# A two-layer fp32 transformer trunk on one core: the low part of twelve weight tiles by an accumulating transfer, a tenth Strassen pair, and one shared PE visit

## The chip, the cores and the metric

The kernel runs on one core of one Trainium2 chip. The metric is the device time of one execution in microseconds (us), as the median of several runs; lower is better. A core has a matrix engine (PE, with its weight loads listed as PEld), three engines for elementwise work (VectorE = DVE, ScalarE = ACT, GpSimd = POOL), a queue engine that starts loads (SyncE = SP), and 16 DMA engines. Each engine works through its own list of instructions in order, and waits for semaphores of the others.

## The reference

An input of 256 tokens by 1024 features goes through two layers; all of it is float32.

```
for i in range(DEPTH):                      # DEPTH = 2
    if i == 0: mix = moba_attention(h, ...) # 16 heads of 64; one block of 256, so plain causal attention here
    else:      mix = dilated_attention(h, ...)   # 3 groups of 4 heads: dilation 1, 4, 16, windows 128, 512, 2048
    h = layer_norm(ALPHA * h + mix, ...)
    h = layer_norm(ALPHA * h + square(relu(h @ w_in)) @ w_out, ...)   # w_in 1024x4096, w_out 4096x1024
```

Each attention has its q, k and v projections, rotary turns of q and k, scores, a softmax, the weighted sum of v (PV) and an output projection.

## The kernel before

**Arithmetic.** A float32 product is made of three products of fp32r parts: each operand is split into a high part (`hi`, a rounded copy) and a low part (`lo = x - hi`), and hi·hi + lo·hi + hi·lo is summed in PSUM. So every weight tile needs three things before PE can read it: its load, a copy to `whi`, and a subtraction into `wlo`.

**Weights.** A weight tile is 128x1024 float32, 512 KB. `load_w` (L402) starts its load on SP into a slot of `raw` (6 slots), has ACT make `whi` (L377, in `split`), and then has DVE make `wlo` as `raw - whi` (L382). `whi` and `wlo` have ten slots each (`NSLOT`), and in the first MLP chunks may also borrow the slots of the LayerNorm tiles `g` and `b`.

**MLP.** The 4096 hidden columns are taken in eight chunks of 512 (chunk 0 has a token-major head of its own). A chunk loads four tiles of `w_in`, `mm_wide` fills four PSUM tiles `tp`, and `relu_sq_T` makes the squared ReLU of them on ACT and DVE, split again into `ahi` and `alo` (or into `rhi`/`rlo` and `v`/`e`/`pt`, which are lent as homes). The products with `w_out` run in two blocks per layer, after chunk 3 and after chunk 7, and add into four PSUM tiles `acc`. A block is a list of steps (`BLOCKS`, L296): "2A" is chunk 2, first pair of `w_out` tiles, as a Strassen pair; "31" is chunk 3, second pair, plain. A plain tile is 12 matmuls of 128x512 (`mm_rows`, two halves of the tokens by six). A Strassen pair (`load_pair` L858, `mm_pair` L882) forms sums of the two tiles on DVE (`m<-raw,raw`, `raw<-m,raw`, `raw<-raw`), splits each of those, and runs seven products of three matmuls, 21 in place of 24. Its activations need sums too (`side_sums` L829). `settle` (L915) puts the four side tiles together with the residual. The last tiles of a layer (`TAIL`) are held back and run row half by row half, so that the LayerNorm of the first half starts while PE still works on the second.

**Attention.** `score` (L663) runs a PE visit of scores for four heads or head groups; `turned` (L718) transposes the softmax on PE (L729); `pv_causal` (L759) and `pv_dilated` (L794) run a PE visit of PV; `attn_out` (L749) copies its result into `ahi` and `alo`. In layer 0 the PV of one unit is already run at the start of the next unit's `score` visit. In layer 1 the PV of each of the two units is a visit of its own. The order of the steps is written out in `ORDER0` and `ORDER1`.

**LayerNorm.** `ln_half` (L940) sums and normalises one half of the tokens on DVE and ACT, with a small power on POOL (L1003), and PE transposes the result four blocks at a time (L712) into the tiles `xs` for the next projection.

**Order.** No order is written by hand inside an engine. `Plan` records every operation with a guessed cost, works out a due time for each backwards from PE's order, adds the corrections of `NUDGE` (a table from operation number to a shift of its due time), and schedules a list per engine. SP's loads keep the order in which they were recorded.

Of the kernel before, what the change touches and what calls it, by code (L numbers as in the profile page):

```python
# [29 lines left out]
TAIL = (5, 6, 6, 7)  # L30
NSLOT = 10
TURN = 0.06
DVE1 = (1, 3)
# [5 lines left out]

STAGE_HOME = (("raw", 6),) * 4 + (("g", 1), ("b", 1)) + (("tok", 2),) * 2  # L40
NWARM = 7
# [10 lines left out]

BURST, RATES = 18.0, (380e3, 270e3)


def latency(p, q):
    if p.eng in ("SP", "AQ"):
        return LANDED
    if p.eng == "PE":
        return 0.0 if q.eng == "PE" else PE_OUT  # L60
    return PE_IN if q.eng == "PE" else LATS.get((p.eng, q.eng), LAT)
# [31 lines left out]
class Plan:  # L93
# [47 lines left out]
    def order(self):  # L141
# [76 lines left out]
        while len(done) < total:  # L218
# [40 lines left out]
            for b in o.bufs:  # L259
                if o.eng != "PE":  # L260
                    b.reader = o
                b.left -= 1
                b.last = max(getattr(b, "last", 0.0), o.end + (PE_OUT if o.eng == "PE" else LAT))
                if not b.left:
                    slots[b.tag].append(b.last)
# [29 lines left out]
AHEADLN = (3.0, 1.5, 4.5)  # L295
BLOCKS = ({3: "00 1A 01 1B 2A 31 2B 3A", 7: "4A 4B 5A 51 6A 61 70 71"}, {3: "00 01 1A 1B 2A 2B 3A 3B", 7: "4A 4B 5A 51 6A 61 70 71"})  # L296
WPAIRS = [
# [7 lines left out]
NUDGE = {  # L305
# [7 lines left out]
}  # L313
# [3 lines left out]
def tile_trunk(  # L317
# [41 lines left out]
    def psum(tag):  # L359
        return mk([P, 512], F32, tag, 4, ps_pool)  # L360

    def f32(ap):
        return ap.bitcast(F32)
# [29 lines left out]
    def landing():  # L393
        return mk([P, 1024], F32, "raw", 6)

# [5 lines left out]

    def load_w(src, n=1024):  # L402
        w = W()
        w.raw = landing()
        w.hi, w.lo = slot()
        dma(lambda: w.raw.t[:, :n], src[:, :n], (), [(w.raw, 0)], P * n * 4)
        split(
            n, lambda: w.raw.t[:, :n], lambda: w.hi.t[:, :n], lambda: w.lo.t[:, :n],
            [(w.raw, 0)], [(w.hi, 0)], [(w.lo, 0)], sbuf=True,
        )  # L410
        return w
# [251 lines left out]
    def score(pss, qk, blocks, first=None):  # L663

        hi, lo = qk
        before, needs, extra = first(pss) if first else (lambda: None, [], 0.0)

        def go():
            before()
            for i in range(max(len(bl) for bl in blocks)):  # L670
                for h in range(2):
                    for t, (a, b) in enumerate(((hi, hi), (hi, lo), (lo, hi))):
                        for n, bl in enumerate(blocks):
                            if i >= len(bl):
                                continue
                            qc, kc, off = bl[i]
                            r = slice(32 * n, 32 * n + 32)
                            mm(pss[n].t[:, off : off + kc.stop - kc.start], a.t[r, h, 0, qc], b.t[r, h, 1, kc],
                               h + t == 0, h + t == 3)

        cost = 0.22 + sum(6 * max((bl[i][1].stop - bl[i][1].start) / 2400 + 0.0135, 0.109) for i, bl in
                          enumerate([max(blocks, key=lambda b: b[0][1].stop - b[0][1].start)] * 2))
        op("PE", cost + extra, go, [(t, h) for t in qk for h in range(2)] + needs, pss)
# [34 lines left out]
    def turned(blocks, r, on_dve=(), first=None):  # L718
# [11 lines left out]

        op("PE", 0.2 + extra + TURN * len(blocks), go, list(r) + [ident] + needs, pss)
        pt = mk([P, 16, P], F32, "pt", 1)
# [60 lines left out]

    def pv_dilated(e, v, vcs, ahi, alo, ahead):  # L794
        r = [t for row in e for t in row]

        def blk(h, m, c):
            return lambda: e[m][h].t[:, c : c + P]

        pt = turned(  # L800
            [blk(h, m, kb * P) for kb in range(2) for h in range(2) for m in range(2)]
            + [blk(h, m, c) for c in (S, S + P) for m in range(2) for h in range(2)], r, DVE1,
        )
        o, o2 = psum("tp"), psum("tp")

        def go():
            for kb in range(2):
                weigh(o, 0, v[0][kb], vcs[0], pt, (4 * kb, 4 * kb + 2), S, 0, kb == 0, kb == 1)
            for m in range(2):
                weigh(o, S, v[1][m], vcs[1], pt, (8 + 2 * m, 9 + 2 * m), P, m * P, True, True)  # L810
                weigh(o2, 0, v[2][m], vcs[2], pt, (12 + 2 * m, 13 + 2 * m), P, m * P, True, True)

        op("PE", 0.2 + 2 * 0.432 + 4 * 0.22, go, [t for x in v for t in x] + [pt], [o, o2], ahead=ahead)
        attn_out(o, 0, 2, ahi, alo, 0, False)
        attn_out(o2, 0, 1, ahi, alo, 2, False)
# [264 lines left out]
    class Mlp:  # L1080
# [17 lines left out]
        def rest(self, between):  # L1098
# [20 lines left out]
            def wide_block(steps):  # L1119
# [3 lines left out]
                for c, n in ((int(x[0]), int(x[1], 16) % 10) for x in steps):  # L1123
# [7 lines left out]
                    else:  # L1131
                        for k in range(2):
                            item = ((*chunks[c], j + k), load_w(wout[i][pos + k]), pos + k, nkt)
                            if nkt - pos - k <= ntail:
                                tail.append(item)
                                continue
                            for m in range(2):
                                mm_rows(acc[m], item, m)
# [26 lines left out]
    def layer0(between):  # L1165
# [93 lines left out]
        pieces = [(o, P * i) for i in range(4)]  # L1259
        op("PE", 0.2 + cost, lambda: go(pieces), needs, [o])  # L1260
        causal_out(pieces, *to)
# [19 lines left out]
    def layer1(between):  # L1281
# [3 lines left out]
        quads = (((0, 0), (0, 1)), ((0, 2), (1, 0)), ((1, 1), (1, 2)))  # L1285
        qk, units, seen = {}, {}, [None, None]
        for step, a in (x.split("-") for x in ORDER1.split()):
# [8 lines left out]
            elif step == "s":  # L1296
                blocks, pss = [], []
                for u, gi in quads[n]:
# [6 lines left out]
                    for h in range(2):  # L1305
# [3 lines left out]
                        else:  # L1309
                            blocks.append([(halves[m], halves[m], m * P) for m in range(2)])  # L1310
                score(pss, qk.pop(n), blocks)
                for i, (u, gi) in enumerate(quads[n]):
# [25 lines left out]
            else:  # L1338
                e, st, sm = units[n]
                vs, vcs = [], []  # L1340
                for gi in range(NG):
                    pair = n * NG + gi
                    vs.append(V1[0] if pair < 4 else V1[1])
                    vcs.append(pair * P if pair < 4 else (pair - 4) * P)
                pv_dilated(e, vs, vcs, *attn[n], AHEAD1[n])
        items = [((*attn[j // 3], j % 3), load_w(wo1[j]), j, 6) for j in range(6)]
# [129 lines left out]
```

## Time and profile before

| | before |
|---|---|
| time, median of 3 runs | 546.71 us (546.37 to 547.74) |
| the profiled execution | 546.42 us |
| its span, first to last instruction | 544.6 us |
| PE busy | 535.7 us, 98% |
| DVE busy | 509.1 us, 93% |
| ACT busy | 365.3 us, 67% |
| POOL busy | 8.7 us, 2% |

The span is read as time on an axis that begins with the first instruction; a row of a timeline gives the start on that axis, the length, the engine, the line and the tiles (written<-read), and how many instructions of the kind it joins. Matmuls overlap, so the time of one is read from start to start of the next and not from its length. "tp", "acc", "wlo" and so on are tile names without the number of the buffer.

### The profile page before, as it was taken

What the parts mean: (1) busy time and instruction counts of PE and PEld (TensorE: products, weight loads), DVE (VectorE), ACT (ScalarE), POOL (GpSimd) and SP (SyncE); (2) the same over time, 40 slices, a digit from 0 to 9 for tenths busy, and PEclk for the clock granted to TensorE, in tenths of its full rate; (3) what the DMA queues carried; (4) which work ended last, traced back from release to release, by engine and by line L of the source; (5) the groups of instructions that cost most, each with busy time, mean ns of one, the idle gap of its engine ahead of it and who ended that gap; (6) DMA issues with size and microseconds to landing.
All of it is one profiled execution on the core that took longest, in us unless ns stands there. A gap on an engine that the chain in (4) does not pass through costs nothing.

```text
span 544.6 us, 9103 instructions
## 1 busy us (share of the span) xinstructions
PE 535.7 (98%) x3416; PEld 455.0 (84%) x3416; DVE 509.1 (93%) x866; ACT 365.3 (67%) x599; POOL 8.7 (2%) x13
## 2 busy tenths in 40 slices
PE   8999999999999999999999999999999999999994
PEld 6888888888888888888888988878888888888884
DVE  6899999797999989899999999899899999999997
ACT  6767776477976666796843557555896656888540
POOL 0000000010000000000010000000000000000001
PEclk9999999999999999999999999999999999999998
DMA  8995345738353678444853833455933358942622
GB/s 317 394 319 165 121 149 180 247 120 305 130 181 101 199 284 325 154 123 186 296 206 113 332 122 106 147 189 158 338 123 116 115 156 259 359 156 78 232 77 78
DMA packets 30396, 105.65 MB, mean 194 GB/s; under 512 B 3344, under 2 KB 4368, under 8 KB 30352
## 3 DMA queue, kind: packets, MB, share of 16 engines
q1 hardware_dynamic: 29952, 104.87, 55.6%
q8 instruction: 27, 0.44, 0.3%
q10 hardware_dynamic: 400, 0.20, 0.1%
q14 instruction: 17, 0.14, 0.1%
HBM read 104.01 MB, written 1.05 MB: 193 GB/s over the span
## 4 chain that ended last, share of the span: by engine, by line
PE 97%; DMA 1%; DVE 1%; ACT 0%; issue 0%; SPq 0%; DVEq 0%
PE tp L386 47%; PE acc L386 47%; PE tp L712 1%; PE tp L729 1%; DMA raw<-in_xw_dram 1%; DVE tok L627 0%; ACT whi L377 0%; SPq L373 0%; ACT xs L377 0%; DVE bst L964 0%; DVE tok L620 0%; DVEq L1470 0%; DVE mv L999 0%
## 5 line engine op out<-in xcount | busy, mean ns | idle before, releaser
L377 ACT ACTIVATE whi<-raw 128x1024 fp32r<-128x1024 f32 (+2 forms) x186 | 188.2, 1037 | 56.3 <-PE acc L386 15.7
L382 DVE TENSOR_TENSOR wlo<-raw,whi 128x1024 fp32r<-128x1024 f32 (+2 forms) x186 | 217.1, 1196 | 4.4 <-ACT whi L377 3.9
L386 PE MATMUL tp<-xs,whi 128*128 128x512 f32 x448 | 105.4, 390 | 0.0
L386 PEld LDWEIGHTS tp<-xs,whi 128*128 128x128 f32 x448 | 83.2, 188 | 16.8
L386 PE MATMUL acc<-xs,whi 128*128 128x512 f32 (+1 forms) x240 | 56.4, 380 | 0.8 <-ACT whi L377 0.7
L386 PEld LDWEIGHTS tp<-xs,wlo 128*128 128x128 f32 x448 | 56.0, 191 | 1.3
L386 PE MATMUL tp<-xs,wlo 128*128 128x256 f32 x448 | 56.4, 283 | 0.0
L386 PE MATMUL acc<-whi,ahi 128*128 128x512 f32 (+1 forms) x136 | 53.5, 394 | 0.0
L386 PE MATMUL acc<-wlo,ahi 128*128 128x512 f32 (+1 forms) x136 | 52.9, 389 | 0.0
L386 PEld LDWEIGHTS acc<-xs,whi 128*128 128x128 f32 x240 | 42.8, 188 | 10.3 <-ACT whi L377 1.7
L386 PE MATMUL acc<-whi,alo 128*128 128x512 f32 (+1 forms) x136 | 47.9, 388 | 0.0
L1057 ACT ACTIVATE ta<-tp 128x256 f32<-128x256 f32 x56 | 20.8, 379 | 21.2 <-PE tp L386 19.8
L620 DVE TENSOR_TENSOR ta<-tp,ta 128x256 f32<-128x256 f32 (+1 forms) x60 | 25.4, 437 | 7.9 <-ACT ta L1057 7.5
L386 PE MATMUL acc<-xs,wlo 128*128 128x256 f32 x224 | 31.7, 283 | 0.0
L386 PE MATMUL tp<-whi,e 128*128 128x512 f32 x90 | 31.2, 390 | 0.0
L386 PEld LDWEIGHTS acc<-whi,ahi 128*128 128x128 f32 x136 | 25.5, 188 | 5.5 <-issue 0.3
L386 PEld LDWEIGHTS acc<-whi,alo 128*128 128x128 f32 x136 | 25.5, 188 | 5.3
L386 PEld LDWEIGHTS acc<-xs,wlo 128*128 128x128 f32 x224 | 29.3, 191 | 0.6
L386 PEld LDWEIGHTS acc<-wlo,ahi 128*128 128x128 f32 x136 | 25.6, 188 | 5.0
L386 PE MATMUL acc<-whi,xs 128*128 128x512 f32 (+1 forms) x112 | 28.8, 365 | 0.0
L377 ACT ACTIVATE whi<-m 128x1024 fp32r<-128x1024 f32 x19 | 20.1, 1057 | 10.9 <-DVE m L620 9.2
L698 ACT ACTIVATE e<-e,mx 128x256 f32<-128x256 f32 (+2 forms) x40 | 19.8, 500 | 9.1 <-DVE mx L688 9.1
(151 smaller groups left out, 907.0 us busy)
## 6 DMA issues: line engine op xcount, KB each, us to landing
raw<-in_win_dram SPq DMA_DIRECT2D x64, 512.0 KB, 4.6
raw<-in_wout_dram SPq DMA_DIRECT2D x64, 512.0 KB, 4.5
raw<-in_wqk_dram SPq DMA_DIRECT2D x24, 512.0 KB, 5.9
raw<-in_wo_dram SPq DMA_DIRECT2D x14, 512.0 KB, 4.3
raw<-in_wv_dram SPq DMA_DIRECT2D x8, 512.0 KB, 8.3
g<-in_lng_dram SPq DMA_DIRECT2D x4, 512.0 KB, 7.3
b<-in_lnb_dram SPq DMA_DIRECT2D x4, 512.0 KB, 7.2
raw<-in_wv1a_dram SPq DMA_DIRECT2D x4, 512.0 KB, 5.4
```

Of the source, the lines that this page charges most:

```text
L377: op("ACT", act(n, sbuf=sbuf), lambda: nc.scalar.activation(hi(), src(), AF.Copy), r, whi, keen=keen)
L382: lambda: nc.vector.tensor_tensor(lo(), src(), f32(hi()), op=ALU.subtract), list(r) + list(whi), wlo,
L386: nc.tensor.matmul(out_ap, lhsT, rhs, start=start, stop=stop)
L620: op("DVE", dve(n) + extra, lambda: nc.vector.tensor_tensor(out_ap(), a(), b(), op=alu), r, w)
L698: lambda: nc.scalar.activation(e(), e(), AF.Exp, bias=bias(), scale=-1.0, accum_out=total()), r, w,
L712: nc.tensor.transpose(ps.t[:, c : c + P], src(), ident.t)
L729: nc.tensor.transpose(ps.t[:, 32 * i : 32 * i + 32], src()[c, :], ident.t[c, c])
L1057: op("ACT", act(S), lambda one=one, ps=ps: nc.scalar.activation(one(), ps.t[:, S:], AF.Copy), [ps], [uk[i]])
```

## The change

Four things change.

- **Blocks.** In layer 0 the step "31" becomes "3B", and the order of the last four steps changes. So one more pair of `w_out` tiles is a Strassen pair.
- **`load_w(..., by_dma)`.** For the plain pairs inside the blocks, 12 tiles in all ("00", "01" and "51" of each layer), `wlo` is no longer made by DVE. ACT writes the negated copy `-hi` into `wlo`, and POOL starts a transfer from `raw` to `wlo` in SBUF that adds as it writes. `raw` is held until the transfer has landed.
- **`pv_dilated(..., held)`.** In layer 1 the PV of the first unit is kept back and run at the start of the `score` visit of step "s-2", into the upper halves of three of its four PSUM tiles. `attn_out` then runs on three pieces of 256 columns instead of one of 512 and one of 256.
- **The planner.** Costs and rates that it assumes change, and `NUDGE` is a new table; all rows behind the first PE visits of layer 0 may stand elsewhere.

The counts of instructions by the order of the program: PE's matmul rows are three fewer by the pair; ACT 558 to 574, DVE 860 to 858, POOL 18 to 30, SP 210 to 210.

```diff
 NSLOT = 10
+NRAW = 6
+BY_DMA = (0, 1)
...
-BURST, RATES = 18.0, (380e3, 270e3)
+BURST, RATES = 18.0, (380e3, 340e3)
+SWDGE, ADDING = 0.9, 1.65
...
 def latency(p, q):
-    if p.eng in ("SP", "AQ"):
+    if p.xfer:
         return LANDED
...
-BLOCKS = ({3: "00 1A 01 1B 2A 31 2B 3A", 7: "4A 4B 5A 51 6A 61 70 71"}, {3: "00 01 1A 1B 2A 2B 3A 3B", 7: "4A 4B 5A 51 6A 61 70 71"})
+BLOCKS = ({3: "00 1A 01 1B 2A 2B 3A 3B", 7: "4A 4B 5A 51 6A 61 70 71"}, {3: "00 01 1A 1B 2A 2B 3A 3B", 7: "4A 4B 5A 51 6A 61 70 71"})
...
 NUDGE = {
-    221: 42.3, 258: 3.2, 275: 51.6, 799: 23.2, 810: 29, 890: 31, 1067: -6, 1076: 4.2, 1150: 55.7, 1239: 31.3, 1349:
...
+    389: 7.9, 399: -6.05, 413: 8.1, 422: 21.4, 460: 3.85, 521: 19.65, 523: 2.05, 541: -7.05, 659: -15.65, 660:
...
-    def load_w(src, n=1024):
+    def load_w(src, by_dma=False):
         w = W()
         w.raw = landing()
         w.hi, w.lo = slot()
-        dma(lambda: w.raw.t[:, :n], src[:, :n], (), [(w.raw, 0)], P * n * 4)
-        split(
-            n, lambda: w.raw.t[:, :n], lambda: w.hi.t[:, :n], lambda: w.lo.t[:, :n],
-            [(w.raw, 0)], [(w.hi, 0)], [(w.lo, 0)], sbuf=True,
-        )
+        dma(lambda: w.raw.t, src, (), [(w.raw, 0)], P * 4096)
+        raw, hi, lo = (lambda: w.raw.t), (lambda: w.hi.t), (lambda: w.lo.t)
+        if by_dma:
+            op("ACT", act(1024, sbuf=True), lambda: nc.scalar.activation(hi(), raw(), AF.Copy), [(w.raw, 0)], [(w.hi, 0)])
+            op("ACT", act(1024, sbuf=True), lambda: nc.scalar.activation(lo(), raw(), AF.Copy, scale=-1.0),
+               [(w.raw, 0)], [(w.lo, 0)])
+            op("POOL", SWDGE, lambda: nc.gpsimd.dma_start(f32(lo()), raw(), accum_op=ALU.add),
+               [(w.raw, 0)], [(w.lo, 0)], xfer=P * 4096 * ADDING)
+        else:
+            split(1024, raw, hi, lo, [(w.raw, 0)], [(w.hi, 0)], [(w.lo, 0)], sbuf=True)
         return w
...
-    def pv_dilated(e, v, vcs, ahi, alo, ahead):
+    def pv_dilated(e, v, vcs, ahi, alo, ahead, held):
...
+        needs, cost = [t for x in v for t in x] + [pt], 2 * 0.432 + 4 * 0.22
+        if held is not None:
+            held.append((go, needs, cost, ahi, alo))
+            return
...
-                            item = ((*chunks[c], j + k), load_w(wout[i][pos + k]), pos + k, nkt)
+                            item = ((*chunks[c], j + k), load_w(wout[i][pos + k], k in BY_DMA and nkt - pos > ntail), pos + k, nkt)
...
-                score(pss, qk.pop(n), blocks)
+                if held:
+                    go, needs, cost, *to = held.pop()
+                    pieces = [(ps, S) for ps in pss[:3]]
+                    score(pss, qk.pop(n), blocks, lambda _: (lambda: go(pieces), needs, cost))
+                    for j, piece in enumerate(pieces):
+                        attn_out(*piece, 1, *to, j, False)
+                else:
+                    score(pss, qk.pop(n), blocks)
...
-                pv_dilated(e, vs, vcs, *attn[n], AHEAD1[n])
+                pv_dilated(e, vs, vcs, *attn[n], AHEAD1[n], held if n == 0 else None)
```

Three places show how rows move. The first is PE at the LayerNorm of layer 1's attention, first half of the tokens (`tok_123`): the rows at the end of the output projection (`acc`), the LayerNorm's transposes, and the first rows of the MLP that read `xs`. Before:

```order
L386 MATMUL acc_749_4288<-whi_744_3973,ahi_608_4292 128x512
L386 MATMUL acc_749_4288<-wlo_745_4264,ahi_608_4292 128x512
L386 MATMUL acc_749_4288<-whi_744_3973,alo_609_4298 128x512
L712 MATMUL tp_753_4374<-ident_49_87,tok_123_345 128x128 x4
L712 MATMUL tp_754_4381<-ident_49_87,tok_123_345 128x128 x4
L386 MATMUL tp_769_4390<-whi_756_4004,xs0_1_75 128x512
```

And the same place of the changed program:

```order
L717 MATMUL tp_758_4395<-ident_49_87,tok_123_342 128x128 x4
L386 MATMUL acc_754_4321<-whi_749_3995,ahi_615_4311 128x512
L386 MATMUL acc_754_4321<-wlo_750_4263,ahi_615_4311 128x512
L386 MATMUL acc_754_4321<-whi_749_3995,alo_616_4317 128x512
L717 MATMUL tp_759_4406<-ident_49_87,tok_123_342 128x128 x4
L386 MATMUL tp_774_4414<-whi_761_4029,xs0_1_75 128x512
```

The last three matmuls of the projection, which were ahead of both groups of transposes, now stand between them.

The second place is PE in layer 1 where the first unit's PV runs (`tp<-pt,v`). Before, it stands between rows of the v projection (`acc<-whi,xs`), and the scores of step "s-2" (`tp<-rhi`) come a dozen rows later:

```order
L386 MATMUL acc_719_3975<-wlo_702_3735,xs0_1_75 128x256
L386 MATMUL tp_713_4006<-pt_712_3979,v_599_3385 64x256 x2
L386 MATMUL tp_713_4006<-pt_712_3979,v_699_3990 64x256 x2
L386 MATMUL tp_713_4006<-pt_712_3979,v_599_3385 64x128 x2
L386 MATMUL tp_714_4013<-pt_712_3979,v_599_3385 64x128 x2
L386 MATMUL tp_713_4006<-pt_712_3979,v_699_3990 64x128 x2
L386 MATMUL tp_714_4013<-pt_712_3979,v_699_3990 64x128 x2
L386 MATMUL acc_719_3975<-whi_701_3672,xs0_1_75 128x256
```

Changed:

```order
L386 MATMUL acc_713_4002<-whi_711_3669,xs1_2_76 128x256 x4
L386 MATMUL tp_720_4041<-pt_719_4005,v_606_3407 64x256 x2
L386 MATMUL tp_720_4041<-pt_719_4005,v_706_4009 64x256 x2
L386 MATMUL tp_721_4046<-pt_719_4005,v_606_3407 64x128 x2
L386 MATMUL tp_722_4049<-pt_719_4005,v_606_3407 64x128 x2
L386 MATMUL tp_721_4046<-pt_719_4005,v_706_4009 64x128 x2
L386 MATMUL tp_722_4049<-pt_719_4005,v_706_4009 64x128 x2
L386 MATMUL tp_720_4041<-rhi_691_3998 128x128
L386 MATMUL tp_721_4046<-rhi_691_3998 128x128
```

The scores follow the PV directly and share its PSUM tiles.

The third place is ACT in the second block of layer 1, where the two tiles of "51" are made ready (`raw_1076` and `raw_1079`); L409 is the copy, L410 the negated copy:

```order
L409 ACTIVATE whi_1077_5751<-raw_1076_5628 128x1024
L1065 ACTIVATE ta_1037_5763<-tp_1032_5618 128x256
L1065 ACTIVATE ta_1037_5763<-tp_1033_5630 128x256
L1067 ACTIVATE ta_1037_5763<-ta_1037_5763 128x2x256
L409 ACTIVATE whi_1080_5782<-raw_1079_5645 128x1024
L377 ACTIVATE e_1013_5790<-ta_1012_5592 128x512
L410 ACTIVATE wlo_1078_5797<-raw_1076_5628 128x1024
L410 ACTIVATE wlo_1081_5802<-raw_1079_5645 128x1024
L1065 ACTIVATE ta_1038_5817<-tp_1035_5683 128x256
```

POOL's transfers into `wlo_1078` and `wlo_1081` can start behind these two negated copies; PE reads `wlo_1078` for the first time in this row, 30 matmuls of 128x512 behind the first read of `wlo_1071`, the DVE row that follows the input of `e_1013` directly on DVE:

```order
L386 MATMUL tp_1040_5778<-wlo_1071_5785,e_990_5648 128x512
L386 MATMUL tp_1040_5778<-whi_1070_5728,e_991_5654 128x512
L386 MATMUL acc_786_4905<-whi_1072_5740,ahi_970_5545 128x512
...
L386 MATMUL acc_786_4905<-whi_1077_5751,ahi_970_5545 128x512
L386 MATMUL acc_786_4905<-wlo_1078_5797,ahi_970_5545 128x512
```

Before, the low parts of these two tiles were subtractions on DVE.

More of the change, by code (lines that the diff above doesn't have):

```diff
@@ L38 @@
 NFIRST = 4
-STAGE_HOME = (("raw", 6),) * 4 + (("g", 1), ("b", 1)) + (("tok", 2),) * 2
+STAGE_HOME = (("raw", NRAW),) * 4 + (("g", 1), ("b", 1)) + (("tok", 2),) * 2
 NWARM = 7
@@ L262, in order @@
                 b.left -= 1
-                b.last = max(getattr(b, "last", 0.0), o.end + (PE_OUT if o.eng == "PE" else LAT))
+                b.last = max(getattr(b, "last", 0.0), o.end + (LANDED if o.xfer else PE_OUT if o.eng == "PE" else LAT))
                 if not b.left:
@@ L393, in landing @@
     def landing():
-        return mk([P, 1024], F32, "raw", 6)
+        return mk([P, 1024], F32, "raw", NRAW)
     def slot():
@@ L679, in go @@
                                h + t == 0, h + t == 3)
-        cost = 0.22 + sum(6 * max((bl[i][1].stop - bl[i][1].start) / 2400 + 0.0135, 0.109) for i, bl in
+        cost = 0.42 + sum(6 * max((bl[i][1].stop - bl[i][1].start) / 2400 + 0.0135, 0.109) for i, bl in
                           enumerate([max(blocks, key=lambda b: b[0][1].stop - b[0][1].start)] * 2))
@@ L729, in go @@
                     nc.tensor.transpose(ps.t[:, 32 * i : 32 * i + 32], src()[c, :], ident.t[c, c])
-        op("PE", 0.2 + extra + TURN * len(blocks), go, list(r) + [ident] + needs, pss)
+        op("PE", 0.4 + extra + TURN * len(blocks), go, list(r) + [ident] + needs, pss)
         pt = mk([P, 16, P], F32, "pt", 1)
@@ L803, in pv_dilated, with go @@
         )
-        o, o2 = psum("tp"), psum("tp")
[L806 to L813, printed above, removed]
+        def go(pieces):
+            for kb in range(2):
+                weigh(*pieces[0], v[0][kb], vcs[0], pt, (4 * kb, 4 * kb + 2), S, 0, kb == 0, kb == 1)
+            for m in range(2):
+                for i in (1, 2):
+                    weigh(*pieces[i], v[i][m], vcs[i], pt, (4 + 4 * i + 2 * m, 5 + 4 * i + 2 * m), P, m * P, True, True)
+        needs, cost = [t for x in v for t in x] + [pt], 2 * 0.432 + 4 * 0.22
+        if held is not None:
+            held.append((go, needs, cost, ahi, alo))
+            return
+        o, o2 = psum("tp"), psum("tp")
+        op("PE", 0.4 + cost, lambda: go([(o, 0), (o, S), (o2, 0)]), needs, [o, o2], ahead=ahead)
         attn_out(o, 0, 2, ahi, alo, 0, False)
@@ L1259, in layer0 @@
         pieces = [(o, P * i) for i in range(4)]
-        op("PE", 0.2 + cost, lambda: go(pieces), needs, [o])
+        op("PE", 0.4 + cost, lambda: go(pieces), needs, [o])
         causal_out(pieces, *to)
@@ L1285, in layer1 @@
         quads = (((0, 0), (0, 1)), ((0, 2), (1, 0)), ((1, 1), (1, 2)))
-        qk, units, seen = {}, {}, [None, None]
+        qk, units, seen, held = {}, {}, [None, None], []
         for step, a in (x.split("-") for x in ORDER1.split()):
```

9 rows, old and new, of the table NUDGE are left out of this document.

## The prediction

> **What bounds the kernel now.** I read the page first: busy shares, then the chain that ended last.
>
> ```profile
> span 544.6 us, 9103 instructions
> PE 535.7 (98%) x3416; PEld 455.0 (84%) x3416; DVE 509.1 (93%) x866; ACT 365.3 (67%) x599; POOL 8.7 (2%) x13
> PE 97%; DMA 1%; DVE 1%; ACT 0%; issue 0%; SPq 0%; DVEq 0%
> ```
>
> PE is both the busiest engine and 97% of the chain. DVE at 93% is close behind, which matters only where it makes PE wait. So the next view is a window from PE's first real product to its last.
>
> ```profile
> 8.04:537.39 529.35, 529.24 (x3385) 451.07 (x3385) 501.57 (x847) 361.79 (x593) 6.92 (x7) 1.00 0.56 195
> ```
>
> The columns are the length, PE, PEld, DVE, ACT, POOL, granted clock, DMA share. Of 529.35 us PE shows 0.11 idle, at a granted clock of 1.00. Ahead of it lie 8.04 us until the first input is there, behind it 544.6 - 537.39 = 7.2 us of the last LayerNorm half. The rows of both programs are the same in these two pieces, so the time goes with the length of PE's list plus whatever PE waits inside it. A matmul's row overlaps the next, so a short wait hides in "busy"; the spacing of starts tells it. The unit of price is in the chain:
>
> ```profile
> 176.67 0.68 PE tp L386 x3
> ```
>
> Three matmuls of 128x512 take 0.68 us, 0.227 each. Against that spacing I went through PE's timeline in order of time. The visible waits are at the LayerNorms' transposes:
>
> ```profile
> 117.20 0.60 PE L712 MATMUL tp<-ident,tok 128*128 128x128 f32 x4
> 117.56 0.48 PE L386 MATMUL tp<-whi,xs 128*128 128x512 f32 x1
> 117.87 0.60 PE L712 MATMUL tp<-ident,tok 128*128 128x128 f32 x4
> 118.49 0.51 PE L386 MATMUL tp<-whi,xs 128*128 128x512 f32 x1
> ...
> 289.36 1.03 PE L712 MATMUL tp<-ident,tok 128*128 128x128 f32 x8
> 290.31 0.96 PE L386 MATMUL acc<-whi,xs 128*128 128x512 f32 x3
> ...
> 364.67 1.29 PE L712 MATMUL tp<-ident,tok 128*128 128x128 f32 x8
> 366.01 0.50 PE L386 MATMUL tp<-whi,xs 128*128 128x512 f32 x1
> ```
>
> Four transposes without a wait take 0.36 from start to the next start (117.20 to 117.56); so eight should take 0.72. The second four take 0.62 (0.26 too many), the eight at 289.36 take 0.95 (0.23 too many), the eight at 364.67 take 1.34 (0.62 too many). Together 1.11 us. At 364.67 the row behind them reads `xs`, which ACT writes late, since two weight copies are ahead of it in its queue:
>
> ```profile
> 363.46 2.01 ACT L377 ACTIVATE whi<-raw 128x1024 fp32r<-128x1024 f32 x2 [4.17 <-PE acc L386]
> 365.38 0.57 ACT L377 ACTIVATE xs<-tp 128x512 fp32r<-128x512 f32 x1
> ```
>
> **The change part by part.** *The tenth pair* takes 24 matmuls to 21: 3 x 0.227 = **-0.68 us**, on PE's list and so on the end.
>
> *The shared visit.* What a visit costs beyond its matmuls is in the timeline of layer 1:
>
> ```profile
> 337.06 0.28 PE L386 MATMUL acc<-wlo,xs 128*128 128x256 f32 x1
> 337.27 1.96 PE L386 MATMUL tp<-pt,v 128*64 128x256 f32 x24
> 339.15 0.39 PE L386 MATMUL acc<-whi,xs 128*128 128x256 f32 x1
> 339.38 0.28 PE L386 MATMUL acc<-wlo,xs 128*128 128x256 f32 x1
> 339.49 0.28 PE L386 MATMUL acc<-whi,xs 128*128 128x256 f32 x1
> ```
>
> Rows of 256 columns follow each other by 0.12 or 0.11 (339.38, 339.49); into the visit it takes 0.21 (337.06 to 337.27), out of it 0.23 (339.15 to 339.38). So a visit costs 0.09 + 0.11 = 0.20 in changes of shape, and one visit fewer is **-0.20 us**. The change from PV to scores inside the visit could give back between 0 and all of it; layer 0 already joins them without a row of its own for that, so I take the whole.
>
> *The LayerNorms.* The order of rows splits two groups of eight into fours with other PE work between them (layer 1's attention LayerNorm is shown above: three matmuls, 0.68 us, between) and puts more rows ahead of the others. At 364.67 the wait was 0.62, less than the 0.68 of the inserted rows; at 289.36 it was 0.23 and there are now several matmuls; at 117.87 it was 0.26, and by the count of rows since the last row of the projection the second transposes come some two matmuls (0.44) later. Each wait is shorter than what now covers it: **-1.11 us**. If the transposes only move with their input, nothing is gained: the bound on the other side is 0. I take the full gain, since the LayerNorm's own work on DVE is the same. Each split costs a change of shape: up to 0.20 by the visit above, near 0 by the x4 group above (its 0.36 holds its entry); three splits, **+0.10**.
>
> *DVE.* What the pair adds and the transfers take away:
>
> ```profile
> L382 DVE TENSOR_TENSOR wlo<-raw,whi 128x1024 fp32r<-128x1024 f32 x180 | 214.2, 1219 | 3.9 <-ACT whi L377 3.5
> L382 DVE TENSOR_TENSOR wlo<-m,whi 128x1024 fp32r<-128x1024 f32 x19 | 23.2, 1220 | 0.1
> L620 DVE TENSOR_TENSOR m<-raw,raw 128x1024 f32<-128x1024 f32 x19 | 23.2, 1219 | 0.0
> L620 DVE TENSOR_TENSOR raw<-raw 128x512 f32<-128x512 f32 x19 | 13.0, 686 | 0.1
> L620 DVE TENSOR_TENSOR raw<-m,raw 128x512 f32<-128x512 f32 x19 | 13.0, 686 | 0.0
> L382 DVE TENSOR_TENSOR v<-raw,v 128x512 fp32r<-128x512 f32 x19 | 12.9, 686 | 0.8 <-ACT v L377 0.8
> L382 DVE TENSOR_TENSOR e<-ta,e 128x512 fp32r<-128x512 f32 x15 | 10.3, 687 | 0.2
> L620 DVE TENSOR_TENSOR ta<-ta 128x128 f32<-128x128 f32 x38 | 10.9, 288 | 0.7
> L620 DVE TENSOR_TENSOR ta<-ta 128x256 f32<-128x256 f32 x19 | 8.0, 420 | 0.2
> ```
>
> A pair needs 1.22 + 1.22 + 3 x 0.686 + 0.687 + 2 x 0.288 + 0.42 = 6.2 us of DVE; twelve subtractions fewer are 12 x 1.219 = 14.6. DVE ends some 8.4 us lighter, about 92%. None of that is on the end by itself. ACT gains twelve negated copies, and about 2.3 us for the pair:
>
> ```profile
> L377 ACT ACTIVATE whi<-raw 128x1024 fp32r<-128x1024 f32 x180 | 185.4, 1056 | 52.7 <-PE acc L386 15.7 <-DMA raw<-in_win_dram 8.3 <-issue 6.8
> ```
>
> 12 x 1.056 + 2.3 = 15 us: 365 becomes 380 of 544, 70%. Cover is PE's list. Where it is gone is seen by how near DVE already runs to PE in layer 1's second MLP:
>
> ```profile
> 500.82 1.22 DVE L382 TENSOR_TENSOR wlo<-raw,whi 128x1024 fp32r<-128x1024 f32 x1
> ...
> 502.52 0.39 PE L386 MATMUL tp<-wlo,ahi 128*128 128x512 f32 x1
> ```
>
> This low part is done at 502.04 and read at 502.52: half a microsecond to spare, without a wait. All rows there have a new order, so some such place may come up short. Before has none in the MLPs, so 0 is the near end; the far end I set at 2 us, twice the LayerNorms' waits; I take **+0.4**, near the row.
>
> *The transfers.* This trace has no accumulating transfer. The nearest rows are the loads of the same size:
>
> ```profile
> raw<-in_wout_dram SPq DMA_DIRECT2D x64, 512.0 KB, 4.5
> raw<-in_wo_dram SPq DMA_DIRECT2D x14, 512.0 KB, 4.3
> raw<-in_wv_dram SPq DMA_DIRECT2D x8, 512.0 KB, 8.3
> ```
>
> From issue to landing 4.3 to 8.3 us; I take 4.5, the same tiles' own load. Queued behind the wait: on POOL only later transfers (the next LayerNorm's power stands behind the block's last transfer, which lands before PE is through with it); on SP the twelve loads that need a `raw` slot held by a transfer, and all loads behind them. Only 8.3 of the 52.7 us that ACT idles before its copies was ended by the loads of `w_in`, so loads mostly run ahead, and I cost that at 0. PE waits if its cover is shorter than the transfer. The eight tiles of "00" and "01" are made long before their step. Tightest are the tiles of "51". In layer 1 the negated copy ends about when DVE ends `wlo_1071` (ACT's `e` and negated copy beside DVE's subtraction), and PE reads `wlo_1078` 30 matmuls behind `wlo_1071`: 30 x 0.227 = 6.8 us. In layer 0 PE reads `wlo_553` 25 matmuls (5.7 us) after `whi_547`, whose copy ended at least one DVE subtraction (1.2) sooner, and two ACT copies (2.1) lie between: at least 4.8 us. At 4.5 both are covered: **0**. At 8.3 they would be short by 1.5 and up to 3.5.
>
> The Trainium skill, "DMA: Bandwidth & Descriptors", section "Anatomy of one DMA — SWDGE (gpsimd) path", fits a transfer issued by GpSimd as 2.0 us plus bytes over 436 GB/s, by which an estimate for 512 KB is 3.2 us, less than each row here; no run here shows it yet, and the fit is not said to be of one that adds. By it the sum would be the same 0.
>
> The sum from the profiled execution: 546.42 - 0.68 - 0.20 - 1.11 + 0.10 + 0.4 = 544.93. That execution was 0.29 below the median of 546.71, within the spread of the three runs. **I predict 544.9**, for the likeliest case 543.9 to 545.6.
>
> **The rivals.** *(1) Only the list gets shorter.* The LayerNorm's waits move with their input or come back at new places: 546.42 - 0.68 - 0.20 = 545.5, with the small stalls 545.9, and by the median's offset up to 546.2. For it: the same DVE work is in front of the transposes, and ACT has more copies that can stand ahead of `xs`, as at 363.46. Against it: the inserted rows are as long as the waits were.
>
> *(2) The transfer is slower than its cover.* If a transfer that reads and adds takes t us to land, PE waits t - 6.8 at layer 1's "51" and t - 4.8 (at most) at layer 0's. Slower begins 0.3% or 1.64 us above the median (about what a measurement of this kernel can tell from no change), at 548.35, so at 3.4 us of waits: t of 7.5 if layer 0's cover is its least, 9 if it is as long as 8. At t = 12 the waits are 5.2 and 4 to 7: 554 to 557. For it: the wv loads took 8.3, and DMA is at 0.56 of its engines; it has to read where it writes, and POOL issues it. Against it: the other two rows quoted are 4.3 and 4.5, the latter the load of these very tiles. The Trainium skill, "SBUF — State Buffer", section "Who interferes with whom", gives a way into it: GpSimd, which writes the descriptors, is locked out while a DVE copy or tensor_scalar holds the ports they share in a two-port mode. By that page tensor_tensor has no such mode, and DVE's rows quoted above for the blocks are TENSOR_TENSOR, so by it the lock is rare at "51"; no run here shows it.
>
> *(3) DVE or ACT falls behind in layer 1.* The new order leaves less to spare than the half microsecond at 502.04: two or three waits of one subtraction each (1.22) give 544.5 + 2.4 to 3.7 = 547 to 548.2, no change that can be told.
>
> **How the numbers follow.** Forecast 0.52, (1) 0.25, (2) 0.13, (3) 0.10. Most of the forecast's own range, and little else, lies more than 0.3% (545.07) below the median: faster 0.45. Its upper end, (1), most of (3) and a mild (2) are within 0.3%: 0.41. The rest of (2) and a little of (3) are slower: 0.14. The range of 543.9 to 548.4 takes in the forecast, (1), (3) and a mild (2); what it leaves out is most of (2) and the odd better case.
>
> **What would show it.** PE's count of matmuls three fewer. One row of 24 PV matmuls that runs into the scores without rows of `acc` between. The transposes of layer 1's attention LayerNorm as two groups of four, each 0.36 to the next start. Transfers into `wlo` that land in about 4.5 us, and no gap of PE at "51". DVE near 501 us, ACT near 380. I am wrong if PE's idle time in its window grows beyond a microsecond, above all with a DMA as its releaser, or if the transposes still take 0.6 to 1.3 us.

## The result, and the profile after

| | before | changed |
|---|---|---|
| median | 546.54 us (546.10 to 547.74, 6 runs) | 550.4 us (549.88 to 551.21, 6 runs) |
| ratio | | 1.0071, 95% interval 1.006 to 1.0083 |
| profiled execution, its span | 546.42, 544.6 us | 550.36, 548.3 us |

The change makes the kernel 0.7% slower, some 3.9 us. The forecast was 544.9 us, in a range up to 548.4.

The page of the changed kernel, its busy shares, the chain that ended last, and two rows of its DMA issues (the last column is the median from issue to landing):

```profile
span 548.3 us, 9149 instructions
PE 535.8 (98%) x3413; PEld 453.7 (83%) x3413; DVE 502.4 (92%) x864; ACT 378.4 (69%) x615; POOL 18.8 (3%) x25
PE 75%; DVE 10%; DMA 6%; ACT 4%; issue 3%; SPq 0%; POOL 0%; DVEq 0%; ACTq 0%
...
raw<-in_wout_dram SPq DMA_DIRECT2D x64, 512.0 KB, 4.8
...
wlo<-raw POOLq DMA_DIRECT2D x12, 512.0 KB, 8.0
```

PE has three matmuls fewer, DVE went from 509.1 to 502.4, ACT from 365.3 to 378.4: the sizes forecast. But PE is only 75% of the chain now, and DMA and DVE have entered it. The window from PE's first real product to its last says the same:

```profile
7.83:540.66 532.83, 529.39 (x3382) 449.72 (x3382) 494.93 (x845) 374.96 (x609) 17.02 (x19) 1.00 0.61 205
```

It is 3.48 us longer than before (529.35), at the same clock, and PE is idle 3.44 us of it, where it was 0.11. Behind the window lie 7.6 us, where it was 7.2: DVE's last row ends 3.54 us ahead of the end of the span, 3.15 before. In the later runs of this program it is 3.46 to 3.54 wherever there are transfers, short ones too, and 3.14 in the one that has none. So some 0.4 us at the end come with the transfers; the prediction had this piece unchanged.

What PE waited for, from the view of its waits (total, times, longest):

```profile
PE acc L386 <- DMA wlo<-raw: 2.4, 1, 2.4
PE tp L386 <- PEq L1476: 0.8, 1, 0.8
PE acc L386 <- ACT whi L377: 0.6, 1, 0.6
PE tp L717 <- DVE tok L632: 0.5, 1, 0.5
PE tp L717 <- issue: 0.4, 1, 0.4
PE tp L386 <- ACT ta L934: 0.2, 1, 0.2
```

The 0.8 is the start, as before. The largest is a transfer. PE's timeline there, in step "51" of layer 1:

```profile
513.78 0.39 PE L386 MATMUL acc<-whi,ahi 128*128 128x512 f32 x1
516.56 0.50 PE L386 MATMUL acc<-wlo,ahi 128*128 128x512 f32 x1 [2.39 <-DMA wlo<-raw]
516.89 0.39 PE L386 MATMUL acc<-whi,ahi 128*128 128x512 f32 x1
```

From start to start 2.78 and then 0.33 in place of twice 0.227: 2.66 us lost at one row. It is the second tile of the step, `wlo_1081`. The chain of waits shows its transfer, and the row of SP an issue right behind its landing:

```profile
505.33 11.19 DMA wlo<-raw
516.51 0.04 issue
516.56 2.79 PE acc L386 x11
```

```profile
516.53 0.33 SPq L373 DMA_DIRECT2D raw<-in_wout_dram  x1
```

The transfer took 11.19 us and landed at 516.51 (505.33 + 11.19); 0.02 us later SP could issue the load that needed the `raw` slot. The first tile's transfer, issued at 504.38, took 6.7 and landed as PE came to it; SP's next load went out at that moment, too. In layer 0 the two transfers of "51" took 7.0 and 8.7 us and landed in time, but the loads behind them went out only then (257.26 and 260.48) and were late. ACT's timeline shows it, and PE's some 15 us later, at the LayerNorm of the first MLP:

```profile
264.17 1.06 ACT L377 ACTIVATE whi<-raw 128x1024 fp32r<-128x1024 f32 x1 [1.32 <-DMA raw<-in_wout_dram]
266.82 1.06 ACT L377 ACTIVATE whi<-raw 128x1024 fp32r<-128x1024 f32 x1 [1.59 <-DMA raw<-in_wout_dram]
```

```profile
280.80 0.39 PE L386 MATMUL acc<-whi,alo 128*128 128x512 f32 x1
281.67 0.66 PE L717 MATMUL tp<-ident,tok 128*128 128x128 f32 x4 [0.48 <-DVE tok L632]
282.08 0.48 PE L386 MATMUL acc<-whi,rhi 128*128 128x512 f32 x1
```

0.87 from start to start in place of 0.23: the LayerNorm's DVE work stood behind subtractions that had waited for loads. That makes two theories. **T**: the accumulating transfers land too late, and cost twice, at the row that reads the low part and by the `raw` slot they hold until they land. **O**: the new order of rows is at fault, and would wait in any case.

### The profile page after: what moved, and what is told of

It reads as the page before. It is cut to its first block, busy times and chain, and to the rows that moved or that the text cites. A ratio compares the mean times of both kernels' runs of the same rounds, so it can differ in the third digit from the quotient of the medians.

```text
span 548.3 us, 9149 instructions
## 1 busy us (share of the span) xinstructions
PE 535.8 (98%) x3413; PEld 453.7 (83%) x3413; DVE 502.4 (92%) x864; ACT 378.4 (69%) x615; POOL 18.8 (3%) x25
## 4 chain that ended last, share of the span: by engine, by line
PE 75%; DVE 10%; DMA 6%; ACT 4%; issue 3%; SPq 0%; POOL 0%; DVEq 0%; ACTq 0%
PE acc L386 37%; PE tp L386 36%; DVE wlo L382 4%; DMA wlo<-raw 4%; ACT whi L377 2%; PE tp L717 1%; DVE raw L625 1%; DMA raw<-in_wout_dram 1%; DVE m L625 1%; PE tp L734 1%; DMA raw<-in_xw_dram 1%; DVE ta L625 1%; DVE tok L632 1%; ACT wlo L410 1%; DVE v L382 0%
## 5 line engine op out<-in xcount | busy, mean ns | idle before, releaser
L377 ACT ACTIVATE whi<-raw 128x1024 fp32r<-128x1024 f32 (+2 forms) x174 | 176.5, 1036 | 64.2 <-DMA raw<-in_win_dram 15.3
L382 DVE TENSOR_TENSOR wlo<-raw,whi 128x1024 fp32r<-128x1024 f32 (+2 forms) x174 | 203.7, 1196 | 11.6 <-ACT whi L377 8.4
L386 PE MATMUL tp<-whi,e 128*128 128x512 f32 x96 | 33.1, 390 | 0.0
L377 ACT ACTIVATE whi<-m 128x1024 fp32r<-128x1024 f32 x20 | 21.2, 1061 | 12.4 <-DVE m L625 12.3
L625 DVE TENSOR_TENSOR m<-raw,raw 128x1024 f32<-128x1024 f32 x20 | 24.4, 1222 | 3.9 <-DMA raw<-in_wout_dram 3.9
L386 PE MATMUL tp<-whi,xs 128*128 128x512 f32 x80 | 25.5, 400 | 0.0
```

What stands on the lines that cost most here:

```text
L377: op("ACT", act(n, sbuf=sbuf), lambda: nc.scalar.activation(hi(), src(), AF.Copy), r, whi, keen=keen)
L382: lambda: nc.vector.tensor_tensor(lo(), src(), f32(hi()), op=ALU.subtract), list(r) + list(whi), wlo,
L386: nc.tensor.matmul(out_ap, lhsT, rhs, start=start, stop=stop)
L625: op("DVE", dve(n) + extra, lambda: nc.vector.tensor_tensor(out_ap(), a(), b(), op=alu), r, w)
```

## The experiments

The reference of every ratio is the kernel before, run beside it on the same chip. In the diffs `load_w(...)` is the call alone, cut out of its line, and a comment behind it names the run.

**1. Short transfers, every row in place.** All twelve, and only the four of step "51":

```diff
-    def load_w(src, by_dma=False):
+    def load_w(src, by_dma=False, cols=1024):
...
-            op("POOL", SWDGE, lambda: nc.gpsimd.dma_start(f32(lo()), raw(), accum_op=ALU.add),
+            op("POOL", SWDGE, lambda: nc.gpsimd.dma_start(f32(lo())[:, :cols], raw()[:, :cols], accum_op=ALU.add),
...
-    load_w(wout[i][pos + k], k in BY_DMA and nkt - pos > ntail)
+    load_w(wout[i][pos + k], k in BY_DMA and nkt - pos > ntail, 64)                       # short_all
+    load_w(wout[i][pos + k], k in BY_DMA and nkt - pos > ntail, 64 if c == 5 else 1024)   # short_51
```

> All rows stay where the changed kernel has them; the twelve accumulating transfers add 64 of the 1024 columns only (the low part of the other columns is left as the negated copy, so part of the low-part product is left out). Theory T, the transfers land too late, at the reading row itself and by the raw slots, loads and subtractions queued behind them: PE's waits at 516.56 (2.66 with the row behind it), at 511.5 (0.1), at the LayerNorm at 281.67 (0.7) and the small ones at 402.6 and 449.8 (0.26 and 0.43) go, 4.2 in all: about 546.2 us. Rival O, the new order makes all waits but the one at the reading row: only 2.8 go, about 547.6, and the LayerNorm at 281.67 still waits. Rival N, PE's wait has another cause than the transfer: above 549.5.

> As the run before, but only the four transfers of the tiles of step 51 add 64 columns; the eight of 00 and 01 are whole. T: the waits at 511.5 and 516.56 and the one of the LayerNorm at 281.67 go, 3.5 in all: about 546.9 us; what it is above the run before is the price of the eight early transfers, 0.7 by T. By O it equals the run before, since the early eight have 12 to 17 us to spare, and both are about 547.6.

short_all: 545.36 us, ratio 0.9975 (0.9961 to 0.9989): faster than before. Its row of DMA issues:

```profile
wlo<-raw POOLq DMA_DIRECT2D x12, 32.0 KB, 3.2
```

And the whole view of PE's waits:

```profile
PE tp L386 <- PEq L1476: 0.8, 1, 0.8
```

Only the start is left. From a ratio of 1.0071 to 0.9975, 5.2 us go with the short transfers, and not one row has moved on any engine. (Only the `raw` slots are dealt out otherwise: in layer 1 the second load behind the first transfer waits for its landing here, the third in the changed kernel.) O falls for the changed kernel as it stands, and N, the rival of another cause, with it.

short_51: 546.31 us, 0.9988 (0.9973 to 1.0003), in runs spread from 544.43 to 547.85. The profiled one is among the slowest (547.68). The LayerNorm at 281 has no wait there, but in layer 1 the two transfers of 32 KB took 7.1 and 6.5 us and held SP's next load until 511.19, so fewer bytes did not make every transfer quick; why is not shown. By the ratios 4.5 of the 5.2 us (1.0071 to 0.9988) belong to the four transfers of "51", as roughly as that spread allows. The 0.7 us left between the two runs is what T gave for the early eight, but the intervals overlap, so that part isn't settled.

The wait at 111.0 (0.57; the 0.4 "issue" of the waits) came and went between profiled executions of one order: none in short_all, 0.34 in short_51. It stands ahead of every transfer; what decides it was not tried. T had put 4.2 us on the transfers, and the profiled executions differ by 4.85 (550.36 to 545.51): most of the rest is this wait, which is not theirs.

**2. The low parts by DVE again**, for step "51" and for all twelve:

```diff
-    load_w(wout[i][pos + k], k in BY_DMA and nkt - pos > ntail)
+    load_w(wout[i][pos + k], k in BY_DMA and c < 4)              # dve_51
...
-BY_DMA = (0, 1)
+BY_DMA = ()                                                      # dve_all
```

> The four tiles of step 51 get their low part by subtraction on DVE again, the eight of 00 and 01 stay with the transfers; the numbers of the table of shifts follow. T: 2.4 us more DVE work in each second block and no transfer to wait for; the LayerNorm at 281.67 waits less, since loads come sooner, so 547 to 548. Rival D, DVE has nothing to spare in the second blocks, which is what the transfers were for: each subtraction shows up as a wait of PE, 549.5 or more.

> No accumulating transfer at all: twelve subtractions on DVE, the tenth pair and the shared visit stay. T: near the run before, 547 to 548.5, since the eight early tiles had time to spare either way. D: DVE is 14.6 us heavier than in the changed kernel (some 517 us, 94%), and the time is above 550.

dve_51: 548.51 us, 1.0039 (1.0022 to 1.0056), between the two theories; its largest wait of PE is on DVE (`xs`, 1.0). dve_all: 551.95 us, 1.0101 (1.0074 to 1.0127): D was right. The busy shares of dve_all:

```profile
PE 536.5 (98%) x3413; PEld 454.9 (83%) x3413; DVE 514.4 (94%) x876; ACT 368.6 (67%) x603; POOL 7.9 (1%) x13
```

And what PE waited for in it (the start and a wait of 0.4 left out):

```profile
PE tp L386 <- DVE ta L625: 2.6, 3, 1.4
PE acc L386 <- DVE wlo L382: 0.9, 2, 0.5
PE acc L386 <- DVE v L382: 0.8, 1, 0.8
```

With this table DVE can't take the twelve back: 4.3 us of waits on DVE. So the transfers do relieve it. By the ratios, and with the few rows that the planner moved between these kernels, transfers that are short save 6.9 us (1.0101 against the 0.9975 of short_all), of which their length takes back 5.2.

**3. The transfer by itself.** A kernel without the reference's work, with nothing but transfers of 512 KB within SBUF:

```diff
+    def add(dst):
+        nc.gpsimd.dma_start(dst, src, accum_op=ALU.add)
...
+    for _ in range(4):
+        add(lo)
+    loads(30)
+    for _ in range(32):
+        nc.vector.tensor_tensor(c, a, b, op=ALU.subtract)
```

> None of the reference's work: 512 KB transfers within SBUF from one tile into another, each waiting for the one before but where said, measured from issue to landing, in this order: four accumulating ones alone; a pair without a wait between; four beside a stream of DVE subtractions of 128x1024 (two SBUF inputs, as in the blocks); four beside a stream of DVE copies of 128x1024; four beside loads of 512 KB, six in flight; four beside loads and subtractions; three plain ones by GpSimd, three plain ones by SP, alone. Theory A, the accumulating transfer is slow by itself: about 6 us alone, as the first of each pair in the trace (5.8 to 6.0), a second behind it 2 to 3 more, and no stream changes that much; a plain one takes 4 to 5. Theory L, it is quick alone (3 to 4.5) and the loads beside it make it 8 to 11: with loads 8 or more. Theory V, DVE's work holds GpSimd up: beside the subtractions 2 us or more longer than alone, or, if only copies do it, beside the copies.

The DMA issues of that kernel, stretch by stretch, in this order: four alone; a pair without a wait between (two rows); four beside subtractions; four beside copies; four beside loads (two rows); four beside loads and subtractions; three plain ones by GpSimd, three by SP.

```profile
lo<-src POOLq DMA_DIRECT2D x4, 512.0 KB, 4.6
...
lo<-src POOLq DMA_DIRECT2D x1, 512.0 KB, 4.6
lob<-src POOLq DMA_DIRECT2D x1, 512.0 KB, 6.6
...
lo<-src POOLq DMA_DIRECT2D x4, 512.0 KB, 4.5
...
lo<-src POOLq DMA_DIRECT2D x4, 512.0 KB, 4.8
...
ring<-in_win_dram SPq DMA_DIRECT2D x23, 512.0 KB, 10.1
lo<-src POOLq DMA_DIRECT2D x4, 512.0 KB, 8.4
...
lo<-src POOLq DMA_DIRECT2D x4, 512.0 KB, 8.5
...
lo<-src POOLq DMA_DIRECT2D x3, 512.0 KB, 2.8
lo<-src SPq DMA_DIRECT2D x3, 512.0 KB, 2.9
```

This is theory L. Alone the accumulating transfer takes 4.5 to 4.6 us (the first of all 5.0), some 1.7 more than a plain one. Beside loads it takes 8.4. The loads beside it take 10.1, and 7.7 at the end of that stretch, where six are still in flight and no transfer is. DVE's subtractions change nothing, its copies 0.2 to 0.3; V falls. The Trainium skill, "SBUF — State Buffer", section "Who interferes with whom", says that copies can lock GpSimd out in a two-port mode, which tensor_tensor does not have. The subtractions agree; of the lock by copies 0.3 us is all that shows. By the Trainium skill's fit for a transfer by GpSimd ("DMA: Bandwidth & Descriptors", section "Anatomy of one DMA — SWDGE (gpsimd) path") an estimate for 512 KB is 3.2 us: near the plain 2.8, not the accumulating 4.6.

In the changed kernel the transfer of 11.2 us ran beside its neighbour and four loads, the one of 6.7 us beside three loads and that neighbour. No stretch here has both a neighbour and loads; added up from these rows (4.6, 2.0 more behind a neighbour, 3.8 more beside loads) an estimate is 10.4. In the trace, fifteen of the sixteen packets that close the transfer of 11.2 were written by 515.30 and the last at 516.22; why it came so late no run shows.

**4. A planner that knows it.** The transfer is assumed to land 10.5 us after its issue (8.9 and the 1.6 that the planner adds), and the table of shifts is chosen anew:

```diff
+SWDGE, ADDING, LANDS = 0.9, 1.65, 8.9
...
+            if o.xfer and o.eng == "POOL":
+                o.end = s + LANDS
```

> The changed kernel's program, but the planner takes the accumulating transfer to land 10.5 us after its issue instead of some 5, and its table of shifts is chosen anew under that assumption. Theory L, the transfers land late because loads share the DMA engines with them, and the changed order left them no time for it: PE's wait at the second tile of step 51 in layer 1 falls from 2.6 us to under 0.7, and the time to 545.5 to 547.5. Rival S, a whole transfer cannot be hidden at step 51, since a low-part slot is taken only after the slots of the tiles ahead of it: the wait comes back in other places and the time stays above 548.5.

551.13 us, 1.0089 (1.0073 to 1.0104). The transfers of "51" now land 2 to 4 us before their first read, and no wait on them is left. S is right all the same that the time stays above 548.5, but the rows below show late loads, not the low-part slots that it named. SP, ACT, DVE and PE of that kernel, in order of time:

```profile
504.88 0.33 SPq L379 DMA_DIRECT2D raw<-in_wout_dram  x1
...
508.81 0.33 SPq L379 DMA_DIRECT2D raw<-in_wout_dram  x1
...
513.60 1.06 ACT L383 ACTIVATE whi<-raw 128x1024 fp32r<-128x1024 f32 x1 [3.52 <-DMA raw<-in_wout_dram]
...
514.69 1.23 DVE L388 TENSOR_TENSOR wlo<-raw,whi 128x1024 fp32r<-128x1024 f32 x1 [3.35 <-ACT whi L383]
...
514.96 1.06 ACT L383 ACTIVATE whi<-raw 128x1024 fp32r<-128x1024 f32 x1 [0.30 <-DMA raw<-in_wout_dram]
...
524.06 0.49 PE L392 MATMUL acc<-v,ahi 128*128 128x512 f32 x1 [2.02 <-ACT v L383]
525.13 0.50 PE L392 MATMUL acc<-v,ahi 128*128 128x512 f32 x1 [0.58 <-DVE v L388]
```

ACT is idle for 3.52 us until a load lands, DVE 3.35 behind ACT, and PE pays 10 us later, at the last pair of the layer. Two loads are late together. The one that ACT's copy at 513.60 waits for is the load of 504.88, which no transfer held back; it was in flight beside both transfers of "51" and landed at 513.52. The next copy, at 514.96, waits for the load of 508.81: a transfer issued at 502.56 that took 6.2 had landed at 508.76, and only then SP could issue it; it landed at 514.88. Whether the transfers do it or the order was asked directly, with short transfers for step "51" in this very order:

```diff
-    load_w(wout[i][pos + k], k in BY_DMA and nkt - pos > ntail)
+    load_w(wout[i][pos + k], k in BY_DMA and nkt - pos > ntail, 64 if c == 5 else 1024)
```

> The rows of replan, where the four transfers of step 51 already land 2 to 4 us before PE reads them; only those four add 64 columns in place of 1024 (the rest of the columns keeps the negated copy, so part of the low-part product is left out). Theory H, a transfer costs by the raw slot that it holds: the loads of the next tiles are issued only as the transfers land, so ACT, DVE and then PE are late behind them (PE's waits of 2.2 and 0.85 at 524 to 525): with short transfers these waits go and the time is 547 to 548.5. Rival O, that wait belongs to the new order itself: it stays, and the time is above 550.

547.07 us, 1.0008 (0.9999 to 1.0018): some four us less, both waits gone. The forecast of H came true, and O falls here too: the transfers cost this without a single wait at the row that reads the low part. That the held slot does it alone, as H has it, is not shown. The row of DMA issues of the load that ACT's longer wait was for, in replan and in replan_short:

```profile
raw<-in_wout_dram SPq DMA_DIRECT2D x1, 512.0 KB, 8.6
raw<-in_wout_dram SPq DMA_DIRECT2D x1, 512.0 KB, 3.5
```

Short transfers free the slot sooner and also leave the loads beside them quicker, and no run parts the two. The profiled execution of replan, at 549.5 the fastest of its four, shows 2.6 us of waits; the rest of the four us is on no trace.

**5. Versions that could beat both.** Step "51" made ready one step sooner; "51" by DVE; its second tile alone by DVE; each with its own table and the assumption of experiment 4:

```diff
+                    if (c, n) == (5, 0):                                                 # ahead_tuned
+                        made = {k: load_w(wout[i][22 + k], True) for k in BY_DMA}
...
+    load_w(wout[i][pos + k], k in BY_DMA and c < 4)                                      # dve51_tuned
+    load_w(wout[i][pos + k], k in BY_DMA and (c < 4 or k == 0 and nkt - pos > ntail))    # one51_tuned
```

> As replan, and in both second blocks the two tiles of step 51 are loaded, copied and put in their slots ahead of the pair 5A, one step sooner; again a table chosen for this. L: the transfers of step 51 are issued 6 us or more sooner against the row that reads them, and land before it; no wait of PE on a transfer, and 544.5 to 546 us, below both kernels. S: above 548.5, as the slots and landing places held longer make DVE late in the pair 5A.

> The tenth pair, the shared visit and the eight early transfers of steps 00 and 01 stay; the four tiles of step 51 go by subtraction on DVE, as in dve_51, and the table of shifts is chosen for that, with 10.5 us from issue to landing assumed. If late transfers of step 51 (at the reading row and by the raw slots) were the whole loss, and the early eight with 12 to 17 us to spare cost little, this is 544.5 to 546, below the kernel before. If the early eight cost by the slots and loads too, or DVE cannot take the four back, it is 547 or more.

> As the run before, but the first tile of step 51 keeps its transfer and only the second is subtracted on DVE; the table is chosen for that. One transfer alone holds one raw slot and lands in some 6 to 7 us; if the loss comes from slots held, it is between the changed kernel and the run before: 545.5 to 548.

| run | median | ratio, 95% interval |
|---|---|---|
| ahead_tuned | 546.38 us | 0.9994 (0.9986 to 1.0003) |
| dve51_tuned | 545.75 us | 0.9981 (0.9972 to 0.999) |
| one51_tuned | 546.97 us | 1.0008 (0.9999 to 1.0017) |

dve51_tuned, as forecast, is faster than both kernels, by 0.2% against before (less than the 0.3% that the prediction took for the least that can be told, but its interval leaves out 1): eight transfers where there is time for them, none at "51". No run has the tenth pair and the shared visit without any transfer and with a table of its own, so whether those eight transfers earn anything is not shown. The waits of PE in dve51_tuned, the start left out:

```profile
PE acc L389 <- ACT whi L380: 0.7, 1, 0.7
PE tp L389 <- DVE ta L628: 0.2, 1, 0.2
```

ahead_tuned has no wait on a transfer either and lies 0.4 us above what L gave it; one51_tuned lies where it was forecast. Since three tables were chosen separately, the differences of 0.6 and 1.2 us to dve51_tuned are not put down to a cause.

## Why the prediction was wrong

- **The pair, the visit and DVE's load: right.** PE has three matmuls fewer, and DVE, forecast at 92%, is at 92%. The shared visit runs from PV into the scores:

```profile
338.14 0.40 PE L386 MATMUL acc<-whi,xs 128*128 128x256 f32 x2
338.47 1.96 PE L386 MATMUL tp<-pt,v 128*64 128x256 f32 x24
340.36 0.33 PE L386 MATMUL tp<-rhi 32*128 32x128 f32 x4
```

  The 24 PV matmuls take 1.89 to the first score, against 1.88 to the next `acc` row before; the join cost nothing, so by these rows the saving is the 0.20.

- **The LayerNorms: right where it looked.** The eight transposes at 364.67 are two groups of four:

```profile
363.99 0.60 PE L717 MATMUL tp<-ident,tok 128*128 128x128 f32 x4
364.35 0.48 PE L386 MATMUL acc<-whi,ahi 128*128 128x512 f32 x1
364.67 0.39 PE L386 MATMUL acc<-wlo,ahi 128*128 128x512 f32 x1
...
365.13 0.60 PE L717 MATMUL tp<-ident,tok 128*128 128x128 f32 x4
365.48 0.48 PE L386 MATMUL tp<-whi,xs 128*128 128x512 f32 x1
```

  0.36 and 0.35 to the next start, no wait; so too at the other two places (0.36 at 112.17, 0.35 and 0.36 at 289.50 and 290.40). A split costs 0.09 at the row behind it (364.35 to 364.67 is 0.32, not 0.23), so the 0.10 for three was low. Two other LayerNorm groups took the gain away again: at 281.67 the start is 0.64 late, at 111.0 0.57, 1.21 against the 1.11 won.

- **The sum without the transfers: right, in part by luck.** It gave 544.93, and with transfers of 64 columns the same order of rows ran at 545.36. The 0.4 us of small waits in it did not come (short_all waits at the start alone), and the 0.4 at the end of the program, which it lacks, did.

- **"At 4.5 both are covered: 0": this step failed.** 4.5 us is what the transfer takes alone. I took the nearest row by tile, the `w_out` loads, and set the row of 8.3 us for `wv` aside, which was the nearest by circumstance: six of its eight loads were issued with four to seven others in flight, a `w_out` load with one in the median. Measured 8.0 in the median, 6.7 and 11.2 at the place that mattered. The cover of 6.8 us for `wlo_1078` was about right (504.38 to 511.15 on the trace, 6.5 in short_all); the second tile, which I did not price, was the one that waited, 2.66 us.

- **"I cost that at 0", of the loads behind a held slot: this failed too, and is the larger lesson.** That loads run ahead on average (8.3 us of ACT's idle time) says nothing of the second blocks, where SP's loads went out as the transfers landed (511.13, 516.53). In the changed kernel this costs 0.6 us at the LayerNorm. In replan it stands beside loads slowed in flight, another cost that the prediction put at nothing by leaving it out, and no run parts the two.

- **The chances.** Rival (2) had the place right and a chance of 0.13. It had the reading row's wait only. The trace of before held what would have raised it: from 480 us on DVE is busy 56.75 of 57.40 us, so a load that is late there is late for PE.

## What to carry to other kernels

Price a new transfer by rows that were in the same company, not by the nearest in size: from one alone to one beside loads it nearly doubled. A transfer that reads a staging slot costs by the slot as well, and by the loads that it slows, so ask which load needs that slot next, which are in flight beside it, and who is late behind them; here a planner that only learned the landing time moved the wait. Of the versions tried, the best gave such transfers only to tiles that have more time to spare than the worst landing, and left the tight ones to DVE.

## What the runs showed of the hardware

- An accumulating transfer of 512 KB within SBUF took 4.5 to 4.6 us alone (5.0 the first time), a plain one 2.8 by GpSimd and 2.9 by SP. Two issued 0.5 us apart took 4.6 and 6.6: the second landed 2.5 us after the first.
- Loads in flight slow it, from 4.6 to 8.4 us, and it slows them, from 7.7 to 10.1.
- With a sixteenth of the bytes it took 2.1 to 5.6 us in short_all (median 3.2, against 8.0), and 4.5 to 7.1 in short_51.
- A program with such transfers ended 0.3 to 0.4 us later behind its last DVE row, whatever their length.
